# Hybrid trunk layer on one core: the state-space branch in chunks of eight steps, with plain float32 products

## The chip, the core and the metric

The kernel runs on one core of one Trainium2 chip. The metric is the device time of one execution in microseconds (us), lower is better. A core has five engines that work side by side, each through its own instructions in a fixed order: TensorE (PE: matrix products, and PEld, its weight loads), VectorE (DVE), ScalarE (ACT), GpSimd (POOL) and SyncE (SP). SP only issues transfers between the chip's memory and the core; ACT issues a few of them too.

## The reference, cut to what matters

One layer of a diffusion trunk: 512 latent tokens, 256 context tokens, width 1024. The branch that the change touches is the state-space layer: 32 groups of 16 channels with 64 complex states each, run in both directions, started from the final states of the context.

```python
def s5_discretize(lam_re, lam_im, log_step, b_re, b_im, c_re, c_im):
    lam = lax.complex(jnp.minimum(lam_re, -S5_MIN_DECAY), lam_im)
    lam_dt = lam * jnp.exp(log_step)[..., None]
    lam_bar = jnp.exp(lam_dt)
    b_bar = ((lam_bar - 1.0) / lam)[..., None] * lax.complex(b_re, b_im)
    ...

def s5_latent_states(ux, s5p, h0_f, h0_b):
    steps = jnp.arange(1, ux.shape[1] + 1)[:, None, None]
    h_f = diag_scan(lam_bar[0], s5_drive(ux, b_bar[0])) + jnp.exp(lam_dt[0] * steps) * h0_f[:, None]
    h_b = diag_scan(lam_bar[1], jnp.flip(s5_drive(ux, b_bar[1]), 1)) + jnp.exp(lam_dt[1] * steps) * h0_b[:, None]
    return h_f, jnp.flip(h_b, 1)

def s5_output(u, h_f, h_b, c_mat, d_skip, w_glu_a, w_glu_b):
    y = jnp.real(jnp.einsum('blgp,gnp->blgn', h_f, c_mat[0]) + jnp.einsum('blgp,gnp->blgn', h_b, c_mat[1]))
    y = y.reshape(u.shape) + d_skip * u
    g = jax.nn.gelu(y)
    return (g @ w_glu_a) * jax.nn.sigmoid(g @ w_glu_b)
```

Beside it the layer has a short convolution, a neighbourhood attention, gates that merge the three, an output projection and an MLP.

## The kernel before

**Weights and units.** All large weights come as one stream of blocks of 1 MB, two halves of 128x1024 each (`fetch`, line 142, on SP). `wsplit` turns a half into two float32r tiles, a rounded part `wh` (ACT, line 171) and the remainder `wl` (DVE, line 174), so that three fast products (`mm3`, lines 99 to 101) stand for one exact one. The program is a list of units (`unit_list`): cg, xb, uc (4 each), then ga and cv in turn (12), gb (8), gc (8), then q, k, v in four rounds, lb and la, na, wo, and the MLP's m1 and m2. `slot` runs one unit: it splits the weights of the unit two ahead, pumps the side generators twice, and issues the unit's products in two halves, 24 of 512 columns for most units. There are two raw buffers, so a block is fetched when both halves of the block two before it have been split.

**The state-space branch, stage A** (`gen_s5a`). After the parameters (`gen_par`: powers of lambda and the coefficients CF), eight batches of four groups run beside the units xb to ga. Each builds the chunk matrices: POOL forms the input matrix E (lines 540, 558, 565, six operations of 256 elements a partition), DVE the output matrix CA (lines 540, 561, 568, six of the same size), both from one scratch tile `ta`. E is split in two float32r parts, PE forms the lag products `kps` with them (lines 580, 581), and E and CA go to memory (E_d). The lag products then go through memory three times (KF_d and KB_d, kf and kb, K_d), and POOL adds them once (line 603).

**Stage B** (`S5B`, `gen_s5b`). Sixteen pairs of groups go through a pipeline of chunk states. A chunk is four steps, so that there are 192 chunks in all, 64 of the context and 128 of the latent tokens. For pair t: `load`, a transposition of E on PE with four copies on ACT (`transp`), splits of E and of u (`esplit`, `usplit`), a table of rotations (`table`: POOL, DVE, ACT), the chunk inputs on PE (`states`, tile stps), a rotation (`rot1` on DVE, `rot2` on POOL), four scans over 192 chunks (line 711, DVE), the rotation back (`back1` on DVE, `back2` on POOL, tile h), splits of h, CA and the lag matrix (`hsplit`), and the outputs on PE (`outp`, tile yps), copied by ACT and written to Y_d. Two pieces of this generator run in a slot, at a raised priority, so the scheduler places them ahead of the units where it can. The units go no further than ("q", 1) before all 16 pairs are through:

```python
        while gs in gens:
            if UNITS[i] == ("q", 1):
                pump()
                continue
            slot(i)
            i += 1
```

Then the attention begins (tiles sps, ptps, ops), which reads q, k and v.

Of the kernel before, what the change touches and what calls it, by code (L numbers as in the profile page):

```python
# [53 lines left out]
def stream_list():  # L54
    """Halves in the order in which they are read: start, then units with the late modulation tiles."""
    s = []
    for d in range(8):
        s += [("md", d), ("md", 8 + d), ("st", d)]
    units = unit_list()
    late = [("md", 16 + i) for i in range(32)]  # L60
    at = 38
    for i, u in enumerate(units):
        if i >= at and (i - at) % 3 != 2 and late:
            s += late[:2]
            late = late[2:]
        s.append(u)
    assert not late and len(s) % 2 == 0
    return s
# [7 lines left out]
def trunk(tc, xT, ctxT, cond, vecs, wst, s5p, s5bc, dmat, biasA, outT):  # L76
# [27 lines left out]
    with es:  # L104
# [120 lines left out]
        # =====================================================================  # L225
        # S5: parameters, then per batch of four groups E, CA and the lag matrices
        # =====================================================================
        s5 = {}

        def gen_par(pool, keep):  # L230
            n_sl = [0]
            prm = pool.tile([128, 40, G], F32, name="prm")
# [48 lines left out]
            pr, pi = [None] * 5, [None] * 5  # L281
            pr[1], pi[1] = sl(), sl()
            V.tensor_tensor(pr[1], r1, cs, op=MUL)
            V.tensor_tensor(pi[1], r1, sn, op=MUL)
            ph = keep.tile([128, G], F32, name="ph")
            V.tensor_scalar(ph, tht, 4.0 * 0.15915494309189535, None, op0=MUL)
            V.tensor_scalar(k, ph, ROUND, ROUND, op0=ADD, op1=SUB)
            V.tensor_tensor(ph, ph, k, op=SUB)
            r4 = keep.tile([128, G], F32, name="r4")
            V.tensor_tensor(r4, r1, r1, op=MUL)  # L290
            V.tensor_tensor(r4, r4, r4, op=MUL)
            yield

            t1, t2 = sl(), sl()

            def cmul(orr, oi, ar, ai, br, bi):
                V.tensor_tensor(t1, ai, bi, op=MUL)
                V.tensor_tensor(t2, ai, br, op=MUL)
                V.tensor_tensor(orr, ar, br, op=MUL)
                V.tensor_tensor(oi, ar, bi, op=MUL)  # L300
                V.tensor_tensor(orr, orr, t1, op=SUB)
                V.tensor_tensor(oi, oi, t2, op=ADD)

            for i, (x, y) in {2: (1, 1), 3: (2, 1), 4: (2, 2)}.items():
                pr[i], pi[i] = sl(), sl()
                cmul(pr[i], pi[i], pr[x], pi[x], pr[y], pi[y])
                yield
            # q = (lam_bar - 1) / lam
            den, nr, qr, qi = sl(), sl(), sl(), sl()
# [4 lines left out]
            V.tensor_scalar(nr, pr[1], 1.0, None, op0=SUB)  # L314
            V.tensor_scalar(t2, lim, -1.0, None, op0=MUL)
            yield
            nl = sl()
            V.tensor_copy(nl, t2)
            cmul(qr, qi, nr, pi[1], lre, nl)
            V.tensor_tensor(qr, qr, den, op=MUL)  # L320
            V.tensor_tensor(qi, qi, den, op=MUL)
            yield
            dr, di = [qr], [qi]
            for i in range(1, 4):
                dr.append(sl())
                di.append(sl())
                cmul(dr[i], di[i], qr, qi, pr[i], pi[i])
                yield
            CF = {n: keep.tile([128, G, 4], F32, name="CF" + n) for n in ("cr", "nci", "ncr", "ar", "ai")}
            for s in range(4):  # L330
                for lo_, hi_, e, c in ((0, 64, 3 - s, s + 1), (64, 128, s, 4 - s)):
                    sel = slice(lo_, hi_)
                    V.tensor_copy(CF["cr"][sel, :, s], dr[e][sel])
                    V.tensor_scalar(CF["nci"][sel, :, s], di[e][sel], -1.0, None, op0=MUL)
                    V.tensor_scalar(CF["ncr"][sel, :, s], dr[e][sel], -1.0, None, op0=MUL)
                    V.tensor_copy(CF["ar"][sel, :, s], pr[c][sel])
                    V.tensor_copy(CF["ai"][sel, :, s], pi[c][sel])
                yield
            s5["r4"], s5["ph"], s5["CF"] = r4, ph, CF

        keepp = es.enter_context(tc.tile_pool(name="s5keep", bufs=1))
# [7 lines left out]
        def rms_cols(name, parts, n, pool, cps):  # L349
            """1 / rms of each token: [128 tokens, groups]; parts are squares to be summed over partitions."""  # L350
# [9 lines left out]
        def rms_rows(name, rc, n, pool, ps):  # L360
            """The same along the free axis, on all partitions (in PSUM)."""
# [7 lines left out]
        def modsplit(hi, lo, x, t, A, sh, rs):  # L369
            """hi + lo = x * A * rs + sh"""  # L370
# [17 lines left out]
        # rows of cond, on all partitions  # L388
# [60 lines left out]
        # xa 0..2 in m, xa 3 in s, u 0..3 in a  # L449
# [29 lines left out]
        # scratch in DRAM  # L479
# [1014 lines left out]
```

## Time and profile before

| what | value |
|---|---|
| timed runs | 1111.8, 1113.29, 1119.03 us; median 1113.29 |
| profiled execution, span | 1117.5 us |
| its own time | not listed apart; it lies within the runs' 1111.8 to 1119.03 |
| PE, DVE, ACT, POOL busy | 92, 67, 42, 29 % of the span |
| mean granted clock of TensorE | 0.946 |
| transfers | 142.81 MB in 62760 packets |

The span is the time from the first to the last instruction. A busy PE in this profile is not PE at its peak: products overlap, and a product's duration holds its latency, so that the room it takes is read from the distance of the starts. Idle time of an engine matters only where the chain of waits passes through it. The granted clock is a share of full speed; 1.00 is 2.4 GHz, 0.50 is 1.2 GHz, and means between the two are stretches of either.

### The profile page before, as it was taken

What the parts mean: (1) busy time and instruction counts of PE and PEld (TensorE: products, weight loads), DVE (VectorE), ACT (ScalarE), POOL (GpSimd) and SP (SyncE); (2) the same over time, 40 slices, a digit from 0 to 9 for tenths busy, and PEclk for the clock granted to TensorE, in tenths of its full rate; (3) what the DMA queues carried; (4) which work ended last, traced back from release to release, by engine and by line L of the source; (5) the groups of instructions that cost most, each with busy time, mean ns of one, the idle gap of its engine ahead of it and who ended that gap; (6) DMA issues with size and microseconds to landing.
All of it is one profiled execution on the core that took longest, in us unless ns stands there. A gap on an engine that the chain in (4) does not pass through costs nothing.

```text
span 1117.5 us, 14237 instructions
## 1 busy us (share of the span) xinstructions
PE 1028.6 (92%) x5350; PEld 848.0 (76%) x5350; DVE 749.1 (67%) x1084; ACT 473.8 (42%) x843; POOL 324.2 (29%) x254
## 2 busy tenths in 40 slices
PE   4669978989898898899999999999999999999997
PEld 3448777767676676777887778899888888888887
DVE  8999899628979989977658787756443223443322
ACT  5336543216444535545556554434432112433211
POOL 2771565216877878761010010000000000000000
PEclk9789989998888898899999999999999999999999
DMA  7544156395334353333224355522232323232202
GB/s 267 188 188 151 49 196 217 125 139 182 103 90 142 120 163 133 137 126 138 97 98 146 132 187 172 215 76 81 109 113 76 113 76 113 79 110 88 101 1 76
DMA packets 62760, 142.81 MB, mean 128 GB/s; under 512 B 18194, under 2 KB 40978, under 8 KB 50212
## 3 DMA queue, kind: packets, MB, share of 16 engines
q1 hardware_dynamic: 60788, 138.75, 37.8%
q10 hardware_dynamic: 1904, 3.16, 0.9%
q8 instruction: 42, 0.69, 0.2%
q14 instruction: 26, 0.21, 0.1%
HBM read 125.96 MB, written 15.93 MB: 127 GB/s over the span
## 4 chain that ended last, share of the span: by engine, by line
PE 58%; POOL 9%; DVE 7%; DMA 3%; issue 3%; SPq 2%; ACT 1%; DVEq 0%; POOLq 0%; ACTq 0%
PE m L99 10%; PE m L100 10%; PE m L101 10%; DVE v L711 2%; PE sps L840 2%; POOL v L703 2%; PE ptps L863 1%; PE sps L839 1%; PE wo L100 1%; PE wo L99 1%; PE wo L101 1%; POOL h L726 1%; PE ops L99 1%; POOL h L723 1%; POOL h L725 1%
## 5 line engine op out<-in xcount | busy, mean ns | idle before, releaser
L174 DVE TENSOR_TENSOR wl<-raw,wh 128x1024 fp32r<-128x1024 f32 x144 | 188.9, 1313 | 142.5 <-ACT wh L171 140.6
L171 ACT CAST wh<-raw 128x1024 fp32r<-128x1024 f32 x144 | 150.7, 1047 | 251.1 <-PE m L100 151.1
L99 PE MATMUL m<-rg,wh 128*128 128x512 f32 (+1 forms) x480 | 184.2, 385 | 0.0
L101 PE MATMUL m<-rg,wl 128*128 128x512 f32 (+1 forms) x480 | 183.9, 384 | 0.0
L101 PEld LDWEIGHTS m<-rg,wl 128*128 128x128 f32 x480 | 90.1, 188 | 19.0
L99 PEld LDWEIGHTS m<-rg,wh 128*128 128x128 f32 x480 | 90.0, 188 | 18.7
L100 PE MATMUL m<-rg,wh 128*128 128x512 f32 (+1 forms) x256 | 96.4, 378 | 0.0
L100 PE MATMUL m<-actl,wh 128*128 128x512 f32 x224 | 87.8, 392 | 0.0
L1134 POOL TENSOR_TENSOR junk<-raw,silx 128x1024 f32<-128x1024 f32 x16 | 43.0, 2684 | 138.3 <-DMA raw<-in_wst_dram 138.3
L711 DVE TENSOR_TENSOR_SCAN v<-r,v 128x192 f32<-128x192 f32 x64 | 53.5, 882 | 10.0 <-POOL v L703 7.5
L438 POOL TENSOR_TENSOR prod<-raw,silc 128x1024 f32<-128x1024 f32 x16 | 47.1, 2968 | 35.0 <-ACT prod L447 23.5
L100 PEld LDWEIGHTS m<-rg,wh 128*128 128x128 f32 x256 | 48.0, 188 | 8.6
L100 PEld LDWEIGHTS m<-actl,wh 128*128 128x128 f32 x224 | 42.0, 188 | 9.8
L1089 DVE SCALAR_TENSOR_TENSOR fg<-m,mod,fg 128x512 f32<-128x512 f32 x14 | 10.5, 752 | 52.8 <-PE m L101 52.8
L92 ACT CAST rg<-relu 128x512 fp32r<-128x512 f32 (+1 forms) x36 | 20.3, 575 | 38.6 <-DVE relu L1082 38.6
L93 DVE TENSOR_TENSOR actl<-relu,rg 128x512 fp32r<-128x512 f32 (+1 forms) x36 | 22.3, 633 | 18.5 <-ACT rg L92 18.5
L723 POOL TENSOR_TENSOR h<-A 64x256 f32<-64x256 f32 x16 | 19.7, 1231 | 44.1 <-DVE A L717 44.1
L92 ACT CAST hh<-h 128x512 fp32r<-128x512 f32 x16 | 9.9, 618 | 52.8 <-POOL h L726 52.7
L100 PE MATMUL wo<-rg,wh 128*128 128x256 f32 (+1 forms) x104 | 32.0, 309 | 0.0
L436 DVE SCALAR_TENSOR_TENSOR junk<-raw,silx 128x1024 f32<-128x1024 f32 x16 | 31.8, 1988 | 0.0
L101 PE MATMUL wo<-rg,wl 128*128 128x256 f32 (+1 forms) x104 | 31.7, 306 | 0.0
L99 PE MATMUL wo<-rg,wh 128*128 128x256 f32 (+1 forms) x104 | 31.6, 307 | 0.0
(484 smaller groups left out, 2943.6 us busy)
## 6 DMA issues: line engine op xcount, KB each, us to landing
raw<-in_wst_dram SPq DMA_DIRECT2D x94, 1024.0 KB, 4.9
E_d<-e SPq DMA_DIRECT2D x8, 512.0 KB, 2.9
u<-U_d SPq DMA_DIRECT2D x64, 48.0 KB, 2.1
fg<-in_xT_dram SPq DMA_DIRECT2D x4, 512.0 KB, 5.8
raw<-in_wst_dram SPq DMA_DIRECT2D x4, 512.0 KB, 7.4
U_d<-un SPq DMA_DIRECT2D x4, 512.0 KB, 3.8
bc<-in_s5bc_dram ACTq DMA_DIRECT2D x8, 256.0 KB, 3.0
eb<-E_d SPq DMA_DIRECT2D x16, 128.0 KB, 2.8
```

The lines of the kernel that those rows point to most:

```text
L92: S.copy(hi, src)
L99: PE.matmul(ps, a[0], b[0], start=start, stop=False)
L100: PE.matmul(ps, a[0], b[1], start=False, stop=False)
L101: PE.matmul(ps, a[1], b[0], start=False, stop=stop)
L171: S.copy(a, src)
L174: V.tensor_tensor(b, src, f(a), op=SUB)
L436: jins[d] = V.scalar_tensor_tensor(junk, w, 1.0, silx, op0=MUL, op1=MUL, accum_out=modx[:, h[1]:h[1] + 1])
L438: P.tensor_tensor(pr, w, silc, op=MUL)
L703: P.tensor_tensor(v[:, :, 0], A[:, :, 0], A[:, :, 1], op=SUB)
L711: V.tensor_tensor_scan(v[:, g, c], r4, v[:, g, c], 0.0, op0=MUL, op1=ADD)
L723: P.tensor_tensor(h[0:64, 0], A[0:64, :, 0], A[0:64, :, 1], op=ADD)
L1134: P.tensor_tensor(junk, half(h), silx, op=MUL)
```

## The change

A chunk becomes eight steps, so there are 96 chunks, 32 of the context and 64 of the latent tokens, and four groups go through the pipeline at a time: eight steps of the pipeline (q = 0 to 7) instead of sixteen. The products of the branch take float32 operands as they are: the splits of E, u, h, CA and the lag matrix are gone. E and CA have 512 elements a partition for a batch instead of 256, for POOL and DVE alike. The transpositions of E move from stage B to stage A, and E is stored transposed (E_d), CA apart (C_d). The backward direction reads u reversed instead of having its own copy. The lag matrices are written to one buffer (KT_d) and read from it as they are used; POOL's addition and two of the trips through memory are gone. The parameters' powers are formed by doubling. `outp` runs one step earlier.

```diff
         def gen_s5a(pool):
...
             def prod(eng, out, mat, cf, b):
-                shp = [128, 4, 4, 16]
+                shp = [128, 4, 8, 16]
...
-                ebh = pool.tile([128, 512], F32R, tag="ebh", name=f"ebh{b}")
-                ebl = pool.tile([128, 512], F32R, tag="ebl", name=f"ebl{b}")
-                split(ebh, ebl, e1[:, 0:2].rearrange("p c m -> p (c m)"))
-                nc.sync.dma_start(E_d[b], e1)
...
+                ps = pa(f"etps{b}").rearrange("p (a m) -> p a m", a=8)
+                kps = pss(f"kps{b}")[:, :128].rearrange("p (g m) -> p g m", g=4)
                 for g in range(4):
                     for c in range(2):
-                        eh, el = (t[:, 256 * c + 64 * g:256 * c + 64 * g + 64] for t in (ebh, ebl))
-                        cg = cm[:, 4 * c + g]
-                        PE.matmul(kps[:, g], eh, cg, start=c == 0, stop=False)
-                        PE.matmul(kps[:, g, 0], el, cg[:, 0], start=False, stop=c == 1)
+                        PE.transpose(ps[:, 2 * g + c], e1[:, c, 128 * g:128 * g + 128], ident)
+                for g in range(4):
+                    for c in range(2):
+                        PE.matmul(kps[:, g], e1[:, c, 128 * g:128 * g + 128], cm[:, 4 * c + g], start=c == 0, stop=c == 1)
+                et = pool.tile([128, 8, 128], F32, tag="et", bufs=1, name=f"et{b}")
+                S.copy(et, ps)
+                nc.sync.dma_start(E_d[b], et)
+                S.copy(kev[:, 4 * b:4 * b + 4], kps)
...
+            nc.sync.dma_start(kf0, kev[112:128, :, 0:16])
             yield
+            V.tensor_tensor(kf0, kf0, dmt, op=ADD)
+            V.tensor_tensor(kev[0:16, :, 16:32], kev[0:16, :, 16:32], kf0, op=ADD)
+            for s in range(8):
+                if s < 7:
+                    nc.sync.dma_start(KT_d[:, :, 16 * (14 - s):16 * (15 - s)].rearrange("g n m -> n g m"), kev[16 * s:16 * s + 16, :, 0:16])
+                nc.sync.dma_start(KT_d[:, :, 16 * (7 - s):16 * (8 - s)].rearrange("g n m -> n g m"), kev[16 * s:16 * s + 16, :, 16:32])
...
-            P.tensor_tensor(kf, kf, kb, op=ADD)
-            yield
-            nc.sync.dma_start(K_d, kf)
...
             def load(self, q):
...
+                et = self.tl("et", q, [128, 8, 128], bufs=2)
+                nc.sync.dma_start(et, E_d[q])
+                u = self.tl("u", q, [128, 4, 128], bufs=4)
+                for s in range(8):
+                    nc.sync.dma_start(u[16 * s:16 * s + 16], U_d[s, 64 * q:64 * q + 64].rearrange("(g n) m -> n g m", n=16))
             def load2(self, q):
...
+                ca = self.tl("ca", q, [128, 2, 4, 128], bufs=1)
+                nc.sync.dma_start(ca.rearrange("p c g m -> p (c g m)"), C_d[q].rearrange("p c m -> p (c m)"))
+                ks = self.tl("ks", q, [128, 4, 128], bufs=1)
+                for s in range(8):
+                    nc.sync.dma_start(ks[16 * s:16 * s + 16], KT_d[4 * q:4 * q + 4, :, 16 * (7 - s):16 * (7 - s) + 128].rearrange("g n m -> n g m"))
...
             def states(self, q):
...
+                        PE.matmul(o[0:64], w[:, 0:64], u[:, g, 0:96], start=True, stop=True, skip_group_check=True)
+                        PE.matmul(o[64:128], w[:, 64:128], u[:, g, 127:31:-1], start=True, stop=True, skip_group_check=True)
...
             def scan(self, q):
                 v = self.t["v", q]
-                for g in range(2):
-                    r4 = s5["r4"][:, 2 * q + g:2 * q + g + 1].to_broadcast([128, 192])
+                for g in range(4):
+                    r8 = s5["r8"][:, 4 * q + g:4 * q + g + 1].to_broadcast([128, 96])
                     for c in range(2):
-                        V.tensor_tensor_scan(v[:, g, c], r4, v[:, g, c], 0.0, op0=MUL, op1=ADD)
+                        V.tensor_tensor_scan(v[:, g, c], r8, v[:, g, c], 0.0, op0=MUL, op1=ADD)
...
             def outp(self, q):
...
+                for g in range(4):
+                    PE.matmul(ps[:, g], ks[:, g], u[:, g, 32:96], start=True, stop=False)
                     for c in range(2):
...
+                        PE.matmul(ps[:, g], ca[:, c, g], h[:, c, g], start=False, stop=c == 1)
+                y = late["y"].tile([128, 4, 64], F32, tag="yd", bufs=1, name=f"y{q}")
+                S.copy(y, ps)
+                for s in range(8):
+                    nc.sync.dma_start(Y_d[64 * q:64 * q + 64, s].rearrange("(g n) m -> n g m", n=16), y[16 * s:16 * s + 16])
         def gen_s5b(sb):
-            """Two pieces to a slot; at step t pair t has its states computed."""
-            ok = lambda q: 0 <= q < 16
-            for t in range(-2, 19):
+            ok = lambda q: 0 <= q < 8
+            for t in range(-2, 11):
...
-                if ok(t - 2):
-                    sb.outp(t - 2)
+                if ok(t - 1):
+                    sb.outp(t - 1)
                 if ok(t + 1):
-                    sb.esplit(t + 1)
-                    sb.usplit(t + 1)
                     sb.table(t + 1)
-                if ok(t - 1):
-                    sb.hsplit(t - 1)
                 yield
```

POOL's order in stage A, one of the eight batches of before and one of after (e is a batch's E, ta the scratch tile, bc the loaded B and C, CF the coefficients):

```order
L540 TENSOR_TENSOR e_1381<-bc_1299,CFnci 128x256
L540 TENSOR_TENSOR ta_1382<-bc_1299,CFncr 128x256
L540 TENSOR_TENSOR e_1381<-bc_1299,CFcr 128x256
L540 TENSOR_TENSOR ta_1382<-bc_1299,CFnci 128x256
L565 TENSOR_TENSOR e_1381<-e_1381,ta_1382 128x256
L558 TENSOR_TENSOR e_1381<-e_1381,ta_1382 128x256
```

```order
L538 TENSOR_TENSOR e_1063<-bc_1003,CFcr 128x512
L538 TENSOR_TENSOR e_1063<-bc_1003,CFnci 128x512
L538 TENSOR_TENSOR ta_1065<-bc_1003,CFnci 128x512
L556 TENSOR_TENSOR e_1063<-e_1063,ta_1065 128x512
L538 TENSOR_TENSOR ta_1065<-bc_1003,CFcr 128x512
L563 TENSOR_TENSOR e_1063<-e_1063,ta_1065 128x512
```

The number of operations is the same, each has twice the elements, and the second use of ta now waits for the first addition.

DVE's order in stage B from one group of scans to the next, before and after (v is scanned; A and B are products with the rotation table tb; el, ul, hl and kl are remainders of splits; wl is a unit's weights):

```order
L711 SCALAR_TENSOR_TENSOR v_2265<-r_676,v_2265 128x192 x2
L93 TENSOR_TENSOR ul_2294<-u_1933,uh_2293 128x384
L711 SCALAR_TENSOR_TENSOR v_2265<-r_676,v_2265 128x192 x2
L93 TENSOR_TENSOR hl_2306<-h_2245,hh_2305 128x512
L93 TENSOR_TENSOR kl_2314<-ks_2211,kh_2313 64x128
L717 TENSOR_TENSOR A_2363<-v_2265,tb_2161 128x512
L718 TENSOR_TENSOR B_2364<-v_2265,tb_2161 128x512
L93 TENSOR_TENSOR el_2290<-etf,eh_2289 128x512
L174 TENSOR_TENSOR wl_3656<-raw_3264,wh_3655 128x1024
L677 TENSOR_SCALAR tb_2427<-rr_2426 128x2x192
L697 TENSOR_TENSOR A_2367<-stps_2343,tb_2298 128x768
L698 TENSOR_TENSOR B_2368<-stps_2343,tb_2298 128x768
```

```order
L678 SCALAR_TENSOR_TENSOR v_2166<-r_676,v_2166 128x96 x8
L684 TENSOR_TENSOR A_2265<-v_2166,tb_2065 128x512
L685 TENSOR_TENSOR B_2266<-v_2166,tb_2065 128x512
L174 TENSOR_TENSOR wl_2753<-raw_2654,wh_2752 128x1024
L640 TENSOR_SCALAR tb_2322<-rr_2321 128x4x96
L174 TENSOR_TENSOR wl_2785<-raw_2654,wh_2784 128x1024
L664 TENSOR_TENSOR A_2269<-stps_2248,tb_2193 128x384
L665 TENSOR_TENSOR B_2270<-stps_2248,tb_2193 128x384
```

The four remainders are gone from the row of work between two groups of scans; a step now covers four groups instead of two.

On SP, after writes the lag matrices to KT_d by 15 transfers and reads them back as ks by eight transfers for each step, one buffer for ks. The first lag matrices, two E and the inputs of the first four steps stand there ahead of the next block of weights. Counted over the branch, the reads of ks become 64 instead of 16 and the writes to Y_d 64 instead of 32, the reads of u stay 64; SP has 415 transfers in all instead of 340.

## Rows read from the trace of the kernel before

**Rows 1.** Busy time of each engine by stretch of the span.

```profile
core 0: us, PE busy (x) PEld busy (x) DVE busy (x) ACT busy (x) POOL busy (x), PEclk, DMA share, GB/s
...
258.00:478.00 220.00, 191.51 (x982) 155.62 (x981) 200.47 (x237) 110.94 (x253) 170.37 (x140) 0.87 0.42 135
...
500.00:700.00 200.00, 199.72 (x1212) 160.95 (x1211) 144.15 (x197) 109.39 (x200) 24.68 (x9) 0.98 0.41 139
860.00:880.00 20.00, 20.00 (x88) 16.24 (x87) 5.87 (x6) 3.15 (x3) 0.00 (x0) 1.00 0.22 77
740.00:760.00 20.00, 20.00 (x171) 19.95 (x170) 16.68 (x34) 10.27 (x20) 0.00 (x0) 1.00 0.46 155
```

**Rows 2.** Waits of PE, 258 to 478 us: total us, times, longest.

```profile
PE stps L100 <- DVE ul L93: 10.8, 7, 3.6
```

**Rows 3.** Chain of waits, 290 to 325 us, its shares by line.

```profile
by line: issue 18.2%; DVE v L711 17.1%; POOL h L723 13.7%; POOL v L703 11.7%; POOL h L725 11.3%; POOL v L704 6.9%; DVE A L717 5.8%; POOL h L726 5.2%; POOL rr L678 3.7%; POOL h L724 3.3%; DVE ul L93 2.9%; POOL cl L93 1.4%; DVE kl L93 0.8%; D
```

**Rows 4.** Timeline of PE about 220 us and about 477 us.

```profile
start us, us, engine line op out<-in xcount [idle before <-releaser]
...
219.69 0.19 PE L580 MATMUL kps<-cm,ebh 128*64 128x64 f32 x1
...
220.59 0.48 PE L100 MATMUL ga<-rg,wh 128*128 128x512 f32 x1
...
477.36 0.40 PE L99 MATMUL q<-rg,wh 128*128 128x512 f32 x1
```

**Rows 5.** Groups of DVE by form, 240 to 495 us.

```profile
line engine op names shapes xcount | busy us, mean ns | idle before us <-releasers
L711 DVE TENSOR_TENSOR_SCAN v<-r,v 128x192 f32<-128x192 f32 x64 | 53.5, 882 | 10.0 <-POOL v L703 7.5 <-POOL v L704 2.5
...
L93 DVE TENSOR_TENSOR el<-etf,eh 128x512 fp32r<-128x512 f32 x16 | 15.3, 953 | 3.4 <-ACT eh L92 3.4
L697 DVE TENSOR_TENSOR A<-stps,tb 128x768 f32<-128x768 f32 x16 | 15.2, 947 | 0.5 <-PE stps L101 0.4
...
L717 DVE TENSOR_TENSOR A<-v,tb 128x512 f32<-128x512 f32 x16 | 11.0, 688 | 0.3
```

**Rows 6.** Groups of POOL by form, same stretch.

```profile
L703 POOL TENSOR_TENSOR v<-A 128x384 f32<-128x384 f32 x16 | 27.7, 1734 | 1.1 <-DVE A L697 1.1
L723 POOL TENSOR_TENSOR h<-A 64x256 f32<-64x256 f32 x16 | 19.7, 1231 | 44.1 <-DVE A L717 44.1
```

**Rows 7.** Timeline of PE about 745 us, a plain float32 product of 256 columns.

```profile
745.41 0.59 PE L366 MATMUL nps<-n_0dg,ones 128*128 128x256 f32 x2
745.65 0.47 PE L100 MATMUL wo<-rg,wh 128*128 128x256 f32 x1
745.96 0.28 PE L101 MATMUL wo<-rg,wl 128*128 128x256 f32 x1
```

**Rows 8.** Timeline of PE about 740 us, plain products of one column.

```profile
740.13 0.36 PE L354 MATMUL nps<-ones,ss 128*128 128x1 f32 x2
740.35 0.36 PE L354 MATMUL nps<-ones,sq 128*128 128x1 f32 x2
740.58 0.37 PE L99 MATMUL wo<-rg,wh 128*128 128x256 f32 x1
```

**Rows 9.** Timeline of SP's queue, 247 to 254 us: issues of u.

```profile
251.96 2.34 SPq L641 DMA_DIRECT2D u<-U_d  x5
```

**Rows 10.** DMA issues: count, KB each, median us from issue to landing.

```profile
raw<-in_wst_dram SPq DMA_DIRECT2D x94, 1024.0 KB, 4.9
...
u<-U_d SPq DMA_DIRECT2D x64, 48.0 KB, 2.1
```

**Rows 11.** Groups of POOL by form, 139 to 212 us.

```profile
L565 POOL TENSOR_TENSOR e<-e,ta 128x256 f32<-128x256 f32 x8 | 8.9, 1108 | 0.0
...
L540 POOL TENSOR_TENSOR e<-bc,CFcr 128x256 f32<-128x256 f32 x8 | 7.0, 874 | 0.0
```

**Rows 12.** Timeline of POOL from the start of stage A.

```profile
140.22 0.62 POOL L540 TENSOR_TENSOR e<-bc,CFnci 128x256 f32<-128x256 f32 x1 [2.15 <-DMA bc<-in_s5bc_dram]
...
143.85 0.61 POOL L540 TENSOR_TENSOR e<-bc,CFcr 128x256 f32<-128x256 f32 x1
```

**Rows 13.** Groups of POOL by form, 120 to 140 us.

```profile
L994 POOL TENSOR_TENSOR fg<-fg,cw 128x504 f32<-128x504 f32 x6 | 8.7, 1461 | 11.1 <-ACT cw L991 11.1
```

**Rows 14.** Timeline of DVE, the first product of a batch in stage A.

```profile
184.55 0.42 DVE L540 TENSOR_TENSOR e<-bc,CFai 128x256 f32<-128x256 f32 x1 [1.52 <-issue]
```

More of the change, by code (lines that the diff above doesn't have):

```diff
@@ L280, in gen_par @@
             V.tensor_scalar(cs, cs, -2.0, 1.0, op0=MUL, op1=ADD)
[L281 to L284, printed above, removed]
+            wk = tp.tile([128, 768], F32, tag="vt", bufs=1, name="parw")
+            PW = wk[:, 0:512].rearrange("p (c s g) -> p c s g", c=2, s=8)
+            qn, cl, q = (wk[:, 512 + 64 * i:576 + 64 * i].rearrange("p (c g) -> p c g", c=2) for i in range(3))
@@ L285, in gen_par @@
+            CF = {n: keep.tile([128, G, 8], F32, name="CF" + n) for n in ("cr", "nci", "ar", "ai")}
+            tm = [CF[n].rearrange("p g s -> p (g s)") for n in ("ar", "ai")]
+            V.tensor_tensor(PW[:, 0, 0], r1, cs, op=MUL)
+            V.tensor_tensor(PW[:, 1, 0], r1, sn, op=MUL)
             ph = keep.tile([128, G], F32, name="ph")
-            V.tensor_scalar(ph, tht, 4.0 * 0.15915494309189535, None, op0=MUL)
+            V.tensor_scalar(ph, tht, 8.0 * 0.15915494309189535, None, op0=MUL)
@@ L296, in cmul @@
-            def cmul(orr, oi, ar, ai, br, bi):
-                V.tensor_tensor(t1, ai, bi, op=MUL)
-                V.tensor_tensor(t2, ai, br, op=MUL)
+            def cmul(out, A, B, n, sel=slice(None)):
+                (ar, ai), (orr, oi) = A, out
+                m = ar.shape[0]
+                br, bi = (x[:, None, :].to_broadcast([m, n, G]) for x in B)
+                t0, t1 = (t[sel, 0:n * G].rearrange("p (s g) -> p s g", s=n) for t in tm)
+                V.tensor_tensor(t0, ai, bi, op=MUL)
+                V.tensor_tensor(t1, ai, br, op=MUL)
@@ L299, in cmul @@
                 V.tensor_tensor(orr, ar, br, op=MUL)
                 V.tensor_tensor(oi, ar, bi, op=MUL)
[L301 to L306, printed above, removed]
+                V.tensor_tensor(orr, orr, t0, op=SUB)
+                V.tensor_tensor(oi, oi, t1, op=ADD)
@@ L307, in gen_par @@
+            pair = lambda t, e, sel=slice(None): (t[sel, 0, e], t[sel, 1, e])
+            for n in (1, 2, 4):
+                cmul(pair(PW, slice(n, 2 * n)), pair(PW, slice(0, n)), pair(PW, n - 1), n)
                 yield
-            den, nr, qr, qi = sl(), sl(), sl(), sl()
+            t1, den = sl(), sl()
             V.tensor_tensor(t1, lre, lre, op=MUL)
@@ L322, in gen_par @@
-            yield
[L323 to L327, printed above, removed]
-                yield
[L329 to L337, printed above, removed]
+            V.tensor_tensor(cl[:, 0], lre, den, op=MUL)
@@ new lines, in gen_par @@
+            V.scalar_tensor_tensor(cl[:, 1], lim, -1.0, den, op0=MUL, op1=MUL)
+            cmul((q[:, 0:1], q[:, 1:2]), (qn[:, 0:1], qn[:, 1:2]), (cl[:, 0], cl[:, 1]), 1)
+            yield
+            for lo_, hi_, e, o0, o, c in ((0, 64, slice(6, None, -1), 7, slice(0, 7), slice(0, 8)),
+                                          (64, 128, slice(0, 7), 0, slice(1, 8), slice(7, None, -1))):
+                sel = slice(lo_, hi_)
+                sg = lambda n: CF[n][sel].rearrange("p g s -> p s g")
+                cr, ci = sg("cr"), sg("nci")
+                cmul((cr[:, o], ci[:, o]), pair(PW, e, sel), (q[sel, 0], q[sel, 1]), 7, sel)
+                V.tensor_copy(cr[:, o0], q[sel, 0])
+                V.tensor_copy(ci[:, o0], q[sel, 1])
+                V.tensor_scalar(CF["nci"][sel], CF["nci"][sel], -1.0, None, op0=MUL)
+                yield
+                V.tensor_copy(sg("ar"), PW[sel, 0, c])
+                V.tensor_copy(sg("ai"), PW[sel, 1, c])
```

224 lines of the change are left out of this document (71 added, 153 removed).

## The prediction, made before the changed kernel ran

> **What bounds the kernel now.** I read the table of stages first. From 500 us to the end PE does nothing but units and attention, and the change touches none of it, so the question is the stretch from 140 to 478 us. In the dense MLP PE starts 88 products of 512 columns in 20 us, one each 0.227 us, and 171 in 20 us where most have 256, 0.117 us each; the granted clock is 1.00 there [rows 1]. From 258 to 478 us the clock is only 0.87 in the mean, PE is busy for 191.5 of 220 us, and DVE for 200.5 us: 91%, the highest share of any stretch [rows 1]. The waits of PE say on whom: the longest row is the states product waiting for the remainder of a split on DVE [rows 2]. The chain between 290 and 325 us says the same in another way: scans on DVE have 17%, POOL's operations on h and v have most of the rest, PE does not appear [rows 3]. So in stage B PE waits for a loop that DVE and POOL pass through once for each pair of groups: scan, rotate back, combine, next pair. From the last lag product, which is over at 220.59 us, to the first product of unit q1 at 477.36 us it is 256.8 us [rows 4].
>
> **Part 1: stage B, the loop.** Before, a pair costs DVE four scans of 0.882 us, four products with the table of 0.69 to 0.95 us, and four remainders, of which el's 0.953 us is the dearest [rows 5]. After, a step holds eight scans of half the length. No row shows a scan of 96. Half of the row, 0.44 us, and the whole, 0.88 us, bound it; I take 0.5, near the half, because the other DVE rows grow with their length (0.688 us for 512 elements, 0.947 for 768 [rows 5]). On the loop of a step lie the scans (8 x 0.5 = 4.0 us, bounds 3.5 and 7.1), one product back (0.69), four combinations on POOL of unchanged size (4 x 1.23 = 4.9) and the two of the next step's v (at most 2 x 1.73 = 3.5) [rows 5, 6]: 13.1 us, bounds 12.6 and 16.2. There are eight such turns instead of sixteen, 105 us, bounds 101 and 130. The remainders on DVE and their casts on ACT go without a substitute.
>
> **Part 2: what PE then has to do.** With the loop this short PE's own work sets the end. In the changed order 598 products of 512 columns stand between the last lag product and q1 (94 of ga, 48 of cv, 384 of gb and gc, 72 of q, k and v) and 48 of 256 columns: 598 x 0.227 + 48 x 0.117 = 141.4 us.
> To these come the branch's own products. Before has one plain float32 product of 256 columns: it is recorded as two matmuls, and from its start to that of the second product behind it there are 745.96 - 745.41 = 0.55 us, of which 0.12 belong to the product between: 0.43 us [rows 7]. Three split products would take 0.36. So a plain product is not cheaper for each column. But there are fewer columns. A states product has 96, and 0.43 x 96/256 = 0.16 us; the weight loads, 64 columns wide, would allow 0.113 us for two records (16 records of that width in 220.59 - 219.69 us [rows 4]). The sum of both, 0.27, is the upper bound, 0.16 the lower; I take 0.18, near the larger of the two, since loads run beside products in all these rows: 128 x 0.18 = 23 us, bounds 20 and 35. An output product has 64 columns and 128-wide weights: two records of one column take (740.58 - 740.13)/2 = 0.225 us [rows 8], more than the 0.107 that the columns need; 96 x 0.225 = 21.6 us, up to 32 if columns and loads add. Together 141.4 + 23 + 21.6 = 186 us at the full clock.
>
> **Part 3: waits that stay.** First, the way of the lag matrices: one small transfer, an addition on DVE, 15 writes, two reads of ks and 16 reads of u stand on SP ahead of what the first two steps of states need. An issue takes 2.34/5 = 0.47 us there [rows 9] and a landing 2.1 us [rows 10]: 34 x 0.47 + 2 x 2.1 = 20.2 us, against 82 products (18.6 us) that PE has in between: 2 us late. Second, the first outputs wait for a whole turn of the loop from the first states, with some 10 us of products behind the states: 4 us. Third, the last outputs come only 24 products (5.4 us) behind those before them, less than a turn: 6 us. One more for the clock, which drops to 1.2 GHz in stretches where PE waits, as the 0.87 shows [rows 1]. That is 13 us, bounds 0 and 40 (some 3 us for each step and as much again at the start). So 256.8 becomes 186 + 13 = 199 us: **-58 us**, bounds -71 and -31.
>
> **Part 4: stage A.** POOL has six operations a batch as before, of 512 instead of 256 elements, four of them products with coefficients (0.874 us in the mean now) and two additions (1.108) [rows 11]. Now it has pauses between batches; doubled it has hardly any, and since PE's transpositions need its result, it sets the pace. Alone, one of the products takes 0.61 us [rows 12] and twice that is 1.22; twice the mean is 1.75. An addition of 504 elements takes 1.461 [rows 13], twice the mean 2.2. DVE works beside it all the time with its own six, so I go above the middle, to 1.55 and 1.85: 4 x 1.55 + 2 x 1.85 = 9.9 us a batch (bounds 7.8 and 11.4), eight of them 79 us (62 and 91). The first starts at 140.2 as now, since it waits for the load of bc [rows 12]. POOL ends at 219, and PE has its last transpositions and some unit products behind, 6 us: 225 against 220.6 us, **+5 us**, bounds -12 and +17. PE's 64 transpositions and 64 plain lag products (64 x 0.225 = 14 us) lie under POOL's time here; they would cost up to 14 us if POOL were faster than I think, which is why the lower bound will hardly be reached. DVE's part of stage A is no longer: its remainders of E and of the C masks make room for the doubled CA. The parameters become fewer, larger DVE operations while PE is dense with cg; I count them, the changed copies of u and everything behind q1 at nothing.
>
> **The sum.** -58 + 5 = -53 us. The span 1117.5 becomes 1064.5; that span is 4.2 us above the median of the runs, and the same 53 us off the median gives 1060 us.
>
> **The rivals.**
> *Locked ports in stage A.* DVE and POOL could exclude each other: a DVE product takes 0.42 us alone [rows 14] and POOL's 0.874 in the mean against 0.61 alone, which is longer by most of a DVE product's data. If all of both engines' doubled work is in a row, a batch is 9.9 + 6 x 0.52 (the data of a DVE product of 512 elements, by the 0.26 us that 256 more of them take [rows 5]) = 13 us, eight are 104 us, stage A ends 30 us later instead of 5: 1085 us. Against it: POOL's mean stays well under the two lone times' sum of 1.03 us [rows 11, 12, 14]. I give it 0.12.
> The Trainium skill, page "SBUF — State Buffer", section "Who interferes with whom", says of this case that a DVE instruction with two SBUF inputs and a GpSimd instruction that reads SBUF exclude each other for the whole instruction, the one that comes second being blocked fully. By that rule in its full strength the time would be the 1085 us of this rival; the rows just named show the slowing, but not all of it.
>
> *The loop stays the bound.* If scans did not shrink with length and POOL were held up by DVE as at present, a turn could cost more than PE's work for a step, about 165/8 = 20 us. Two rows speak for it (v's 1.73 us and the chain's share of POOL [rows 3, 6]); the bound of 16.2 us speaks against it. At 25 us a turn the gain shrinks to some 15 us: 1098 us. 0.06.
>
> *Plain products cost columns plus loads.* Both upper bounds of part 2: 12 + 10 us more, 1082 us. The fast units' loads are hidden throughout, so 0.08.
>
> *Slower: the weight stream starves behind SP's queue.* Stage B now issues 64 reads of ks one by one, where 16 did, and 64 writes of y, where 32 did. The reads of step q+1 wait on SP until the outputs of step q have freed ks (one buffer), and a block of weights behind them waits too: 17 issues (8 us), a landing of 4.9 us [rows 10], a cast and a remainder, 15 us in all. Two units are split ahead, 11 us of cover, and a further block is in its buffer. Were all cover gone, eight steps at 15 us would give +120: 1180 us. It decides from 53/8 = 6.6 us a step that PE really waits for wl. 0.03.
>
> *More than forecast.* No waits in part 3 and stage A at 70 us: 1060 - 13 - 9 = 1038 us. 0.16.
>
> **How the numbers follow.** The forecast of 1060 us, with some 15 us to either side, has 0.55. The range must reach the locked ports and the dearer products, with half the way on to the loop's 1098, and below to the lower bounds of parts 3 and 4 together (1113 - 71 - 12); it can leave out SP: 1030 to 1093 us. Within 1% (11 us, about what a measurement of this kernel tells from no change) or slower lies only what hits the loop's upper part and SP: faster 0.93, same 0.04, slower 0.03.
>
> **What would show it.** Right: q1's first product near 425 us, a clock of 0.95 or more between stage A's end and q1, PE's waits there under 20 us, DVE well under 70%, POOL without pauses between 140 and 215 us. Wrong: scans that keep 0.88 us; states records further apart than 0.1 us at the full clock; POOL batches over 12 us; PE waiting for wl or a raw block; a clock under 0.9 in stage B although PE has work.

## The result: 42 us less, where 53 were forecast

The changed kernel took 1073.16 us in the median of four runs (1071.68 to 1075.22); the kernel before had 1115.44 us over the runs taken with it. The ratio is 0.962, with an interval of 0.959 to 0.965. The profiled execution has a span of 1072.3 us against 1117.5, so 45.2 us are to be explained. The marks of the prediction divide them. Timeline of PE, changed kernel, about the last lag product and the first product of unit q1:

```profile
236.73 0.83 PE L576 MATMUL kps<-bc,e 128*128 128x32 f32 x6
237.40 0.47 PE L101 MATMUL ga<-rg,wl 128*128 128x512 f32 x1
...
439.24 0.40 PE L99 MATMUL q<-rg,wh 128*128 128x512 f32 x1
```

| stretch | before | after | difference | forecast |
|---|---|---|---|---|
| start to the end of the last lag product | 220.6 | 237.4 | +16.8 | +5 |
| from there to the first product of q1 | 256.8 | 201.8 | -54.9 | -58 |
| from there to the end | 640.1 | 633.1 | -7.1 | 0 |

So stage B came within 3 us of the forecast, and stage A alone missed it by 12. Behind q1, before still had outputs of the branch (36 products) and a lower clock (0.92 from 477.36 to 500 us, against 1.00 in the first 23 us behind q1 of the changed kernel); no run parts the two. The stretches of the changed kernel (columns as in [rows 1]):

```profile
140.00:180.00 40.00, 32.42 (x194) 29.67 (x194) 36.12 (x31) 13.83 (x20) 33.10 (x22) 0.79 0.60 205
180.00:238.00 58.00, 49.85 (x267) 41.16 (x268) 53.86 (x44) 16.01 (x23) 44.35 (x28) 0.97 0.66 204
...
238.00:439.00 201.00, 185.46 (x1095) 155.71 (x1094) 108.07 (x169) 60.39 (x97) 80.19 (x69) 0.96 0.60 186
```

In stage B DVE is busy for 108.07 of 201 us now, 54% instead of 91%, and the clock is 0.96 instead of 0.87 [rows 1]. In the first 40 us of stage A it is 0.79, with PE busy for 32.42 of 40 us. PE's waits from 121 to 440 us (total, times, longest) say for whom:

```profile
PE etps L573 <- POOL e L556: 13.3, 5, 6.4
PE stps L653 <- DMA u<-U_d: 8.1, 2, 7.1
PE yps L700 <- DMA ks<-KT_d: 3.4, 1, 3.4
PE stps L653 <- DMA ks<-KT_d: 1.9, 1, 1.9
PE etps L573 <- POOL e L563: 1.6, 4, 0.6
```

The wait for DVE's remainders [rows 2] is gone. The largest is now the transposition of E, which waits 14.9 us in all for POOL: stage A. The groups of POOL and one of DVE there, to be read against [rows 11], and the scans of stage B against [rows 5]:

```profile
L556 POOL TENSOR_TENSOR e<-e,ta 128x512 f32<-128x512 f32 x8 | 15.0, 1881 | 0.5
...
L538 POOL TENSOR_TENSOR e<-bc,CFcr 128x512 f32<-128x512 f32 x8 | 12.6, 1578 | 0.0
L538 POOL TENSOR_TENSOR e<-bc,CFnci 128x512 f32<-128x512 f32 x8 | 12.2, 1521 | 5.2 <-DMA bc<-in_s5bc_dram 5.2
L538 POOL TENSOR_TENSOR ta<-bc,CFnci 128x512 f32<-128x512 f32 x8 | 12.1, 1511 | 8.7 <-DVE c L566 8.6
```

```profile
L174 DVE TENSOR_TENSOR wl<-raw,wh 128x1024 fp32r<-128x1024 f32 x17 | 28.2, 1663 | 4.0 <-ACT wh L171 4.0
L538 DVE TENSOR_TENSOR c<-bc,CFar 128x512 f32<-128x512 f32 x8 | 12.7, 1581 | 0.8 <-DMA C_d<-c 0.8
...
L566 DVE TENSOR_TENSOR c<-c,ta 128x512 f32<-128x512 f32 x8 | 5.7, 718 | 0.1
...
L678 DVE TENSOR_TENSOR_SCAN v<-r,v 128x96 f32<-128x96 f32 x64 | 27.9, 502 | 10.7 <-POOL v L670 10.7
```

POOL's products take about 1.5 us, its first addition 1.9, and it waits 8.6 us for DVE's last use of ta. On DVE one of the products takes 1.581 us in the mean and the last addition 0.718, though both have 512 elements. The timeline tells why. POOL and DVE of the changed kernel, single operations:

```profile
145.87 1.50 POOL L538 TENSOR_TENSOR ta<-bc,CFnci 128x512 f32<-128x512 f32 x1
...
168.70 1.05 POOL L538 TENSOR_TENSOR e<-bc,CFcr 128x512 f32<-128x512 f32 x1
```

```profile
213.87 0.69 DVE L538 TENSOR_TENSOR ta<-bc,CFar 128x512 f32<-128x512 f32 x1
...
224.08 1.43 DVE L538 TENSOR_TENSOR ta<-bc,CFar 128x512 f32<-128x512 f32 x1
225.55 0.69 DVE L566 TENSOR_TENSOR c<-c,ta 128x512 f32<-128x512 f32 x1
```

Where DVE rests, POOL needs 1.05 us, beside DVE 1.50; DVE needs 0.69 us in POOL's pauses and 1.43 beside it. One after the other they would take 1.05 + 0.69 = 1.74 us, or 1.02 + 0.60 = 1.62 us by the distances of their starts where each is alone (POOL 168.70 to 169.72 us, DVE 163.53 to 164.13). Side by side each gets through one operation in 1.47 us (POOL's start at 144.40, 145.87 and 147.33 us, DVE's at 143.44, 144.91 and 146.38): each is shut out for most of the other's operation, not for all of it. That is the rival of the locked ports, and the experiments ask how much of it is true.

### The profile page after: what moved, and what is told of

Its sections match the earlier page's. It is cut to its first block, busy times and chain, and to the rows that moved or that the text cites. A ratio compares the mean times of both kernels' runs of the same rounds, so it can differ in the third digit from the quotient of the medians.

```text
span 1072.3 us, 13748 instructions
## 1 busy us (share of the span) xinstructions
PE 997.2 (93%) x5350; PEld 829.4 (77%) x5350; DVE 657.3 (61%) x931; ACT 409.5 (38%) x656; POOL 250.2 (23%) x171
## 4 chain that ended last, share of the span: by engine, by line
PE 70%; DVE 3%; SPq 3%; DMA 2%; POOL 1%; issue 1%; ACT 1%; DVEq 0%; ACTq 0%; POOLq 0%
PE m L99 10%; PE m L100 10%; PE m L101 10%; PE sps L784 2%; PE ptps L807 2%; PE sps L783 1%; PE wo L99 1%; PE wo L100 1%; PE wo L101 1%; PE gc L99 1%; PE gc L101 1%; PE gc L100 1%; PE ops L99 1%; PE yps L702 1%; PE gb L99 1%; PE ops L100 1%
## 5 line engine op out<-in xcount | busy, mean ns | idle before, releaser
L174 DVE TENSOR_TENSOR wl<-raw,wh 128x1024 fp32r<-128x1024 f32 x144 | 195.2, 1357 | 158.0 <-ACT wh L171 155.0
L1081 DVE SCALAR_TENSOR_TENSOR jk<-raw,silx 128x1024 bf16<-128x1024 f32 x16 | 22.1, 1381 | 28.1 <-DMA raw<-in_wst_dram 28.1
L678 DVE TENSOR_TENSOR_SCAN v<-r,v 128x96 f32<-128x96 f32 x64 | 27.9, 502 | 10.7 <-POOL v L670 10.7
L100 PE MATMUL st_a<-rg,wh 128*128 128x512 f32 x32 | 15.8, 493 | 15.9 <-DVE rg L469 15.9
```

The lines of the kernel that those rows point to most:

```text
L100: PE.matmul(ps, a[0], b[1], start=False, stop=False)
L174: V.tensor_tensor(b, src, f(a), op=SUB)
L678: V.tensor_tensor_scan(v[:, g, c], r8, v[:, g, c], 0.0, op0=MUL, op1=ADD)
L1081: V.scalar_tensor_tensor(jk, half(h), 1.0, silx, op0=MUL, op1=MUL, accum_out=modx[:, i:i + 1])
```

## The experiments

Ratios are to the kernel before, on the same chip. The changed kernel has 0.962. Differences between runs on different chips are taken from the ratios.

**Stage A: the shared scratch tile, or the engines themselves?**

```diff
-                ta = pool.tile([128, 2, 512], F32, tag="ta", name=f"ta{b}")
+                tp1 = pool.tile([128, 512], F32, tag="tp1", name=f"tp{b}")
+                tv1 = pool.tile([128, 512], F32, tag="tv1", name=f"tv{b}")
```

> The changed kernel with the scratch tile ta of stage A divided into two tiles of half the size, one for POOL and one for DVE; the arithmetic stays. Theory (the shared tile couples the engines): POOL's first use of ta in a batch waits for DVE's last use in the batch before, 8.6 us in all; with two tiles these pauses go, the last lag product moves from 237 to about 229 us and the time from 1073 to about 1065 us. Rival (DVE and POOL hold each other up at the memory, the pauses are only where that shows): the operations get longer by what the pauses lose, the last lag product stays within 2 us of 237 and the time within 2 us of 1073.

Measured: 1077.64 us, ratio 0.964 (0.960 to 0.968), no change. The pauses for ta went, and the last lag product ended at 231.7 us, 5.6 earlier. POOL now waits longer for the loads of bc (11.8 us instead of 5.2), and PE for u. Waits of PE, kernel with two scratch tiles, from 228 us:

```profile
PE stps L654 <- DMA u<-U_d: 13.8, 3, 7.2
```

DVE's last matrix, whose write stands on SP ahead of the lag matrices, was no earlier, so the first states were not either (257.8 against 256.2 us). Theory and rival are both half right: the tile makes the pauses, and taking them away alone gains nothing. The longer operations that the rival names are not seen: POOL's six take 9.3 us a batch, against 9.5 with one tile.

```diff
-                prod(P, e1[:, 0], B[:, 0], "cr", b)
+                prod(V, e1[:, 0], B[:, 0], "cr", b)
...
```

> The changed kernel with POOL's six operations of a batch of stage A given to DVE, which then does all twelve; POOL does none. Theory (the two engines exclude each other for most of an operation: DVE's operations take 0.69 us where POOL rests and 1.43 to 1.78 where it works): DVE alone needs 12 x 0.69 plus about 1.5 remainders of weights of 1.2 us, some 10.2 us a batch against 11.6 now, so stage A ends no later, about 228 to 237 us, and the time is 1064 to 1073 us. Rival (no exclusion, DVE's 1.5 us are its own): 12 x 1.5 + 1.5 x 2.0 = 21 us a batch, stage A ends 75 us later, the time is about 1150 us.

Measured: 1061.70 us, ratio 0.949 (0.946 to 0.952): 14 us less than the changed kernel, by giving DVE twice the work. Its groups in stage A, 140 to 240 us, and the stretches:

```profile
L174 DVE TENSOR_TENSOR wl<-raw,wh 128x1024 fp32r<-128x1024 f32 x17 | 20.7, 1220 | 0.1
...
L538 DVE TENSOR_TENSOR ta<-bc,CFcr 128x512 f32<-128x512 f32 x8 | 5.5, 689 | 0.1
...
L538 DVE TENSOR_TENSOR c<-bc,CFai 128x512 f32<-128x512 f32 x8 | 5.5, 688 | 6.9 <-DMA C_d<-c 6.9
...
L559 DVE TENSOR_TENSOR c<-c,ta 128x512 f32<-128x512 f32 x8 | 5.5, 687 | 0.0
```

```profile
140.00:180.00 40.00, 36.37 (x236) 31.86 (x236) 33.42 (x48) 16.15 (x24) 2.06 (x2) 1.00 0.78 224
180.00:240.00 60.00, 57.98 (x313) 48.30 (x312) 53.52 (x79) 17.99 (x24) 0.00 (x0) 1.00 0.59 205
```

All products take 0.69 us, the remainders of weights (wl) 1.220 instead of 1.663, DVE is busy no longer than in the changed kernel (86.9 of 100 us against 90.0 of 98), and PE has 94.3 busy us of 100 and a clock of 1.00, where the changed kernel has 84.3 us and 0.90 in the same stretch. The last lag product is as late as it was (239.2 us), but PE has done more units by then: gb begins at 252.1 us instead of 282.0. To part the two causes, POOL was given back its work with nothing depending on it:

```diff
+                pj = pool.tile([128, 2, 512], F32, tag="pj", name=f"pj{b}")
+                prod(P, pj[:, 0], B[:, 0], "cr", b)
+                prod(P, pj[:, 1], B[:, 1], "nci", b)
+                P.tensor_tensor(pj[:, 0], pj[:, 0], pj[:, 1], op=ADD)
...
```

> The changed kernel with all twelve operations of a batch of stage A on DVE, and POOL besides doing the same six operations as in the changed kernel, but into a tile that nothing reads. Nothing waits for POOL; it can only be felt through the memory. Theory (exclusion): each operation of POOL holds DVE up by about the 0.75 us that lie between DVE's 0.69 and 1.43, so the means of DVE's operations rise from 0.69 to about 1.1 us, a batch takes 4 to 5 us more, stage A ends 20 to 40 us later than 239 and the time is 1075 to 1100 us. Rival (what helped was that PE waits for DVE in place of POOL, or the order that the scheduler wrote): DVE's operations stay at 0.69 us and the ratio at 0.949.

Measured: 1096.07 us, ratio 0.980 (0.976 to 0.984), 34 us more. DVE's groups, 140 to 240 us (six of the eight batches lie in it):

```profile
L538 DVE TENSOR_TENSOR c<-bc,CFai 128x512 f32<-128x512 f32 x6 | 7.8, 1292 | 0.9 <-DMA C_d<-c 0.9
...
L538 DVE TENSOR_TENSOR ta<-bc,CFcr 128x512 f32<-128x512 f32 x6 | 6.8, 1133 | 0.1
...
L563 DVE TENSOR_TENSOR e<-e,ta 128x512 f32<-128x512 f32 x6 | 6.2, 1037 | 0.0
```

The same products take 1.0 to 1.3 us, the last lag product ends at 271.3 us. Nothing uses what POOL makes there. Beside the memory only the loads of bc could pass its delay on, since a buffer of bc is free when POOL has read it too, and DVE waits for those 0.7 us in all:

```profile
DVE e L538 <- DMA bc<-in_s5bc_dram: 0.7, 1, 0.7
```

So what the 34 us come from is longer operations on DVE: this shows that the engines hold each other up.

```diff
-                c1 = pool.tile([128, 2, 512], F32, tag="c1", bufs=1, name=f"c1{b}")
+                c1 = pool.tile([128, 2, 512], F32, tag="c1", bufs=2, name=f"c1{b}")
```

> The changed kernel with stage A's products on DVE and two buffers for the tile c1, so that DVE need not wait for the write of C_d (6.9 us in stage A without it). Theory (DVE paces stage A): the last lag product comes 5 to 7 us before 239 us, and the ratio falls from 0.949 to 0.943 to 0.947. Rival (PE was already dense in stage A, so nothing is to be had there): 0.947 to 0.951.

Measured: 1052.23 us, ratio 0.942 (0.938 to 0.946), the best of all runs: 22 us less than the changed kernel. The last lag product ends at 237.1 us, 2 earlier and not 5 to 7, and from 180 to 240 us PE has no pause at all:

```profile
180.00:240.00 60.00, 60.00 (x338) 51.52 (x336) 49.17 (x74) 18.46 (x25) 0.00 (x0) 1.00 0.69 228
240.00:430.00 190.00, 175.51 (x1074) 146.05 (x1072) 115.46 (x174) 62.92 (x102) 81.08 (x70) 0.97 0.61 191
```

Most of what this run gains over the one with a single c1 lies behind stage A: q1 begins at 415.3 us instead of 426.3, with a clock of 0.97 instead of 0.94 from 240 to 427 us. So the theory's mechanism, DVE's pace in stage A, is shown for some 2 us only, and the cause of the rest stays open.

**Stage B: which part of the change frees it?** The kernel before, with plain operands in states and outputs and no splits there, in chunks of four (u with three buffers, h with two):

```diff
-                        mm3(ps[:, g, 192 * c:192 * c + 192], (eh[:, a], el[:, a]), (uh[:, g], ul[:, g]), True, True)
+                        PE.matmul(ps[:, g, 192 * c:192 * c + 192], eh[:, a], us[:, g], start=True, stop=True)
...
```

> The kernel before (chunks of four, sixteen steps) with only one part of the change: states and outputs in stage B take plain float32 operands, the splits of E, u, h, CA and the lag matrix are gone; u has three buffers and h two. Theory (the loop of scan, rotation and combination bounds stage B, and only fewer steps shorten it): a turn still has four scans of 0.88, one product of 0.69, four combinations of 1.23 and two of 1.73 us, 12.6 us, sixteen are 202 us and with some 45 us ahead 247 against 257 now: 10 to 25 us less, about 1095 to 1105 us. Rival (the remainders on DVE were the bound, the chunk is not): they are 55 of DVE's 200 busy us, the time falls by 40 us or more, to 1075 us or less.

Measured: 1096.62 us, ratio 0.981 (0.976 to 0.986): 21 us less than before, half of the 42. But the changed kernel's 42 already hold the 17 us that it lost in stage A, and this kernel loses nothing there. In the profiled execution stage B takes 241.0 us (221.04 to 462.06), 15.8 less than before, where the changed kernel has 54.9 less; another 8.7 us are gained behind q1. What PE waits for in stage B then, the scans, 192 long, and the stretch (columns as in [rows 1]):

```profile
PE yps L735 <- POOL h L722: 13.8, 6, 5.9
```

```profile
L708 DVE TENSOR_TENSOR_SCAN v<-r,v 128x192 f32<-128x192 f32 x57 | 55.1, 1020 | 22.7 <-POOL v L700 22.7
```

```profile
221.00:462.00 241.00, 217.07 (x989) 164.21 (x988) 173.86 (x194) 100.87 (x212) 148.96 (x138) 0.94 0.50 145
```

PE's longest wait is now for POOL's h (17.3 us in all with the row of line 723), so the loop of scans and combinations holds PE up as the theory said, and the rival's 40 us or more did not come. The other 39 us of stage B came only with the longer chunks. No run parts what those bring: the loop has fewer turns, but PE also has less to do (busy for 185.46 us of 201 instead of 217.07 of 241), and the transpositions have left the stage. Does the loop of the changed kernel still matter?

```diff
+                        V.tensor_tensor_scan(w[:, g, c], r8, v[:, g, c], 0.0, op0=MUL, op1=ADD)
                         V.tensor_tensor_scan(v[:, g, c], r8, v[:, g, c], 0.0, op0=MUL, op1=ADD)
```

> The changed kernel with every scan of stage B done twice (the first time into a tile that nothing reads), so that DVE has 64 more scans of 0.50 us, 4 us in each of the eight turns. Theory (PE's own products set the end of stage B now, a turn of the loop has several us of slack): less than a third of the 32 us is seen, the ratio to the kernel before rises from 0.962 by at most 0.009. Rival (the loop of DVE and POOL is still the bound): nearly all of it is seen, 25 to 32 us, ratio 0.985 to 0.991.

Measured: 1080.72 us, ratio 0.967 (0.963 to 0.970): some 5 us more, with intervals that overlap. The extra scans cost DVE 21 us, not 32, since the two of a pair take 0.542 and 0.334 us in the mean instead of twice 0.502. About a quarter of it is seen, far from the rival's 25 to 32 us: the loop has slack.

```diff
-                P.tensor_tensor(v[:, :, 0], A[:, :, 0], A[:, :, 1], op=SUB)
+                V.tensor_tensor(v[:, :, 0], A[:, :, 0], A[:, :, 1], op=SUB)
...
```

> The changed kernel with POOL's six combinations of a step in stage B (two of v, four of h) given to DVE; stage A as it is. Theory (the loop is off the bound): a turn gets shorter by some 5 us, since the combinations take 0.4 to 0.6 us on DVE instead of 1.2 to 1.7 on POOL, and yet the time moves by less than 5 us, ratio 0.958 to 0.966. Rival (the turn of the loop still sets the pace): 15 us or more are gained, ratio below 0.95.

Measured: 1074.74 us, ratio 0.960 (0.957 to 0.964), no change. The loop is shorter and PE does not gain by it. The scans without POOL's work beside them:

```profile
L678 DVE TENSOR_TENSOR_SCAN v<-r,v 128x96 f32<-128x96 f32 x64 | 18.6, 361 | 0.0
```

The same 64 scans take 0.361 us instead of 0.502: the exclusion holds in stage B too, but off the path.

**The wait of 7.1 us for u.** ACT, SP and PE of the changed kernel about 302 us:

```profile
301.14 0.53 ACT L642 ACTIVATE tb<-rr 128x384 f32<-128x384 f32 x1 [2.80 <-POOL rr L641]
...
302.49 0.35 ACT L704 COPY y<-yps 128x256 f32<-128x256 f32 x1
...
302.87 1.71 SPq L706 DMA_DIRECT2D Y_d<-y  x4
304.62 0.42 SPq L625 DMA_DIRECT2D u<-U_d  x1
...
310.73 0.39 PE L653 MATMUL stps<-u,et 128*64 128x96 f32 x1 [7.05 <-DMA u<-U_d]
```

The copy of y stands on ACT behind a table operation that waits for POOL, the reads of u for a later step stand on SP between the writes of y, and PE waits 7.05 us for u. SP itself had waited 6.8 us for y.

```diff
-                S.copy(y, ps)
+                V.tensor_copy(y, ps)
```

> The changed kernel with the copy of the outputs from yps to y done by DVE instead of ACT. Theory (a chain of queues: ACT's copy of y stands behind a table operation that waits for POOL, the writes of y stand on SP between the reads of u, and the states product waits 7.1 us for u): the copy comes at once, the wait of 7.1 us goes, the time falls by 4 to 8 us to about 1067 us. Rival (SP simply has too many transfers to issue, or u waits for its buffer): the wait for u stays and the time is within 2 us of 1073.

Measured: 1076.99 us, ratio 0.963 (0.959 to 0.967), no change. The longest wait for u is 4.4 instead of 7.1 us, and the waits for ks grow from 3.4 to 6.0:

```profile
PE yps L700 <- DMA ks<-KT_d: 6.0, 3, 3.1
PE stps L653 <- DMA u<-U_d: 5.2, 2, 4.4
```

The chain exists, but what is taken from one transfer on SP comes back at the next.

**Other queues and orders, all with stage A on DVE.** First the inputs u of four steps read early, in a pool of their own:

```diff
+        with tc.high_priority(offset=1000):
+            for q in range(4):
+                load_u(q)
```

> The changed kernel with all of stage A's products on DVE and with the inputs u of the first four steps read ahead of the lag matrices on SP's queue, in a pool of their own. Theory (behind the lag products SP's queue, 15 writes and 24 reads in a row, holds up the first states): the waits for u of 3.6 us in all at the first steps go, ratio 0.943 to 0.947 against 0.949 without the early reads. Rival (PE has enough other products there): 0.949 as without.

Measured: 1075.71 us, ratio 0.963 (0.959 to 0.966), 15 us more than without, the opposite of the theory. SP's queue and DVE's waits in stage A, same kernel:

```profile
187.33 7.72 SPq L606 DMA_DIRECT2D u<-U_d  x16
...
195.62 0.38 SPq L567 DMA_DIRECT2D C_d<-c  x1
```

```profile
DVE c L538 <- DMA C_d<-c: 13.0, 3, 7.6
```

The 32 early reads stand ahead of a write of C_d, DVE waits for it (13.0 us in all against 8.7), and PE is busy for 90.5 us from 140 to 240 us instead of 94.3. PE's waits for u are gone, as the theory had it, but behind stage A those for ks are 7.9 us instead of 3.1. How the 15 us divide stays open. The same with POOL's combinations on DVE:

> As the run with early u and stage A on DVE, with POOL's combinations of stage B on DVE as well. Theory (the loop is off the bound, the two engines hold each other up): within 5 us of that run, rather less time than more, ratio 0.938 to 0.947. Rival (DVE becomes the bound of stage B, since it now has some 8 us more of work a step beside the remainders of weights): ratio 0.955 or more.

Measured: 1065.75 us, ratio 0.954 (0.950 to 0.958): 10 us less than the run above, more than expected, and the ratio lies outside both ranges, close to the rival's 0.955. It has the early reads, and stays above the 0.949 of stage A on DVE alone. Why the step from the run above is larger than expected stays open; the order on PE differs between the two as well.

```diff
-                    nc.sync.dma_start(KT_d[:, :, 16 * (14 - s):16 * (15 - s)].rearrange("g n m -> n g m"), kev[16 * s:16 * s + 16, :, 0:16])
+                    nc.scalar.dma_start(KT_d[:, :, 16 * (14 - s):16 * (15 - s)].rearrange("g n m -> n g m"), kev[16 * s:16 * s + 16, :, 0:16])
...
```

> The changed kernel with stage A's products on DVE and the 15 writes of the lag matrices issued by ACT instead of SP, so that the first u and ks leave SP some 8 us earlier. Theory (SP's queue sets the first states): the first states products start about 6 us earlier than at 259 and the ratio falls from 0.949 to 0.943 to 0.946. Rival (PE has other products to do there, and the steps behind are paced by later transfers): 0.947 to 0.951.

Measured: 1067.93 us, ratio 0.956 (0.952 to 0.959), 7 us more. ACT spends 12 us on the issues, and a unit's cast waits behind them:

```profile
239.16 1.13 ACTq L593 DMA_DIRECT2D KT_d<-kev  x2
...
251.31 1.04 ACT L171 CAST wh<-raw 128x1024 fp32r<-128x1024 f32 x1 [12.18 <-DMA KT_d<-kev]
```

The first states start at 264.0 us, where without the edit they start at 259.3.

All three edits together (two c1, two ks, writes on ACT):

> The changed kernel with stage A's products on DVE, two buffers of c1 and of ks, and the lag matrices' writes on ACT. If the gains add, the ratio is 0.936 to 0.943; if PE is dense in stage A and the waits behind it are only handed on, it stays at 0.945 to 0.951.

Measured: 1058.89 us, ratio 0.948 (0.944 to 0.951): worse than two c1 alone. Gains don't add where the next queue takes them.

## Where the prediction was right and where it was wrong

**What bounded the kernel before: right.** DVE's remainders and the loop of scans and combinations held PE up. Without the remainders and with chunks of four, stage B became 15.8 us shorter, where the whole change brought 54.9, and PE then waited for the loop's h. That the other 39 us are the loop's is not shown: they came together with PE's smaller work.

**Part 1, right.** The scan of 96 took 0.502 us, forecast 0.5. With the turn forecast at 13 us against some 20 of PE's work the loop should be off the path; both runs that lengthened or shortened it say that it is.

**Part 2, one of two terms wrong.** An output product takes 0.217 us (forecast 0.225). A states product was to take 0.18, 0.16 at the least; it takes half, 0.083. PE, changed kernel, outputs and then states:

```profile
370.63 0.33 PE L700 MATMUL yps<-u,ks 128*128 128x64 f32 x2
...
373.23 0.48 PE L99 MATMUL gc<-rg,wh 128*128 128x512 f32 x1
...
354.63 0.25 PE L653 MATMUL stps<-u,et 128*64 128x96 f32 x1
354.64 0.25 PE L654 MATMUL stps<-u,et 128*64 128x96 f32 x1
354.72 0.25 PE L653 MATMUL stps<-u,et 128*64 128x96 f32 x1
...
354.96 0.25 PE L653 MATMUL stps<-u,et 128*64 128x96 f32 x1
```

Twelve output products lie between 370.63 and 373.23 us. The two halves of a states product, lines 653 and 654, start 0.01 us apart, and a pair of them, with two records each, takes (354.96 - 354.63)/2 = 0.165 us: 128 products take 10.6 us, not 23.

**Part 3, too small by about as much.** PE's own work is then 141.4 + 10.6 + 20.8 = 172.8 us of 201.8, so that 29 us are waits and clock, not 13. Of the waits, 13.4 us are for u and ks, which SP issues one by one between the writes of y; the other 15.6 us, the clock of 0.96 among them, are not divided. The rival of SP's queue had this mechanism, but the victims are u and ks, not the weights, and the size is far from +120.

**Part 4, the step that failed.** The forecast took POOL's durations at 9.9 us a batch; they came to 9.5. What failed is the pauses: doubled, POOL was to have "hardly any", and DVE's side was left out ("DVE's part of stage A is no longer"). In fact POOL waited 8.6 us for ta, which one tile lets go only when DVE is done with its part, and 5.2 us for bc; it started at 142.88 instead of 140.22 us. DVE was late because its 0.69 us became 1.43 and more beside POOL. From 142.88 to POOL's last end at 233.27 a batch took 11.3 us, between the 9.9 of the forecast and the 13 of the locked ports: a batch has six of POOL's operations, and DVE is held up by those that it meets. The rule of the Trainium skill (page "SBUF — State Buffer", section "Who interferes with whom") that was weighed there is borne out by the trace, 0.69 against 1.43 us, and by the dummy run; its price at full strength, 13 us a batch and 1085 us, was too much: the batch took 11.3 us, and two operations side by side take 1.47 us instead of 1.62.

**The sum.** +16.8 for +5, -54.9 for -58, -7.1 for nothing. The direction and the range held. That stage B came within 3 us is luck: the two misses of parts 2 and 3, 13 us too much and 16 too little, cancel, which the time alone would not have told. Of the signs named ahead, the clock, DVE's share and PE's waits under 20 us came; q1 near 425 us (439.24) and POOL without pauses did not.

## What to carry to other kernels

When two engines share an elementwise stage, compare an operation's duration beside the other engine with its duration alone before giving each half: here one engine with all of the work beat both by 14 us, and with a second buffer by 22. Work of an engine that nobody waits for is not free either. Before a transfer is moved on a queue, read what will stand behind it: none of the three moves tried here (y's copy, the early u, the writes on ACT) made the kernel faster, and behind each a new wait came up.

## What was not expected of the hardware

Two plain float32 products with 64-wide weights that go to different halves of the output's partitions run side by side: a pair of 96 columns takes 0.165 us, where a single product of 256 columns takes 0.43 [rows 7], which is 0.16 for 96 as an estimate by length. No run here has one half alone. The Trainium skill, page "TensorEngine Tiling (Array Packing)", section "Key Properties", says that tiles of the array work independently, and for a small dimension of up to 64 gives up to twice the speed (section "Theoretical Speedup"); the trace agrees, and the forecast had not used it. And the hold-up between POOL and DVE reaches the scans: 0.361 us in the mean when POOL's combinations are taken away, 0.502 with them.
